# Moving the splits of w_out and the z weights to another stage, halving the z product, and laying out attention's buffers anew

## The chip, the core and the metric

The kernel runs on one core of a Trainium2 chip, as one launch. The metric is the device time in microseconds. A core has a matrix engine (TensorE, in the profile PE for its products and PEld for its weight loads), a vector engine (VectorE, DVE), a scalar engine (ScalarE, ACT), a general engine (GpSimd, POOL) and a fifth engine, SyncE (SP), whose queue in this kernel does little but issue DMA transfers. Each engine executes its own queue of instructions in the order written there, and waits at an instruction until what it needs is there. SBUF is the on-chip memory, in 128 partitions; PSUM is the small memory that takes the products of TensorE, in 8 banks of 128 x 512 fp32.

## What is computed

One hybrid decoder layer on x, 1024 rows of 1024 values in fp32, with a hidden width of 2816 in its two feed-forward networks:

```python
x = layer_norm(DN_ALPHA * x + 0.5 * swiglu(x, ffn1_wg, ffn1_wu, ffn1_wd), ln1_g, ln1_b)
proj = x @ w_in                                    # 3360 columns
(g_q, g_k, g_v, g_z, ..., n_q, n_kc, ..., n_gate) = jnp.split(proj, offsets, axis=-1)
o_gdn = gdn_mixer(g_q, g_k, g_v, g_z, ...)         # 4 heads of 128: ends in ... * silu(g_z)
o_nsa = nsa_mixer(n_q, n_kc, ...)                  # 8 query heads of 64, 2 key/value heads
mix = jnp.concatenate([o_gdn, o_nsa], axis=-1) @ w_out
x = layer_norm(DN_ALPHA * x + mix, ln2_g, ln2_b)
x = layer_norm(DN_ALPHA * x + 0.5 * swiglu(x, ffn2_wg, ffn2_wu, ffn2_wd), ln3_g, ln3_b)
```

swiglu(x) is (silu(x @ wg) * (x @ wu)) @ wd. The first mixer is a gated DeltaNet in chunks of 64 rows; g_z, 512 columns of the projection, only gates its output. The second is sparse attention with compressed, selected and windowed keys.

## The kernel before

**Products.** An fp32 operand is split into two parts, hi (a cast to the rounded type fp32r on ScalarE) and lo (the difference, on VectorE), and a product of two operands is three matmuls: hi x hi, hi x lo, lo x hi. `split` (line 100 the cast, 103 the difference) does this for the down products and the way out, `prep` (lines 290 and 291) for the weights of the gate and up products. A matmul here is 128 x 128 by 128 x 512.

**First feed-forward, gate and up** (`hidden`, 9 to 439 us in the profile). x @ wg and x @ wu are computed in pairs of 256 hidden columns, p from 0 to 10, with a scheme that needs seven half-size products instead of eight. A pair has a unit for gate and a unit for up; a unit has seven products of twelve matmuls (`u.do(n)`, line 302), in the order 1, 6, 2, 7, 5, 4, 3. A weight block of 1 MB comes by DMA into one of three buffers (`wring`); sums of its quarters are made on POOL or VectorE into eight `st` buffers; `prep` splits quarter or sum into `wh` and `wl`, of which there are seven buffers. Intermediate results live in twelve `ev` tiles of 128 x 512, products in the 8 PSUM banks. The hidden values go out to DRAM as `h`.

**First feed-forward, down** (`ffn`, 439 to 694 us). Again seven products, here n = 1, 6, 5, 3, 2, 7, 4, each over eleven p. For each p, `operands` loads two blocks of 256 KB, h and wd, into a ring of twelve `raw` tiles, splits them (`ah`, `al`, `bh`, `bl`, eight sets of buffers) and `mul` runs twelve matmuls over four banks (line 629). In the products 5, 3, 2 and 7, after every p with p % 4 == 1, one **job** is put in (line 664): twelve in all. A job loads a piece of the z columns of w_in (four jobs) or of w_out (eight), 128 x 1024, over POOL's DMA queue into `jr`, splits it into `jh` and `jl` (lines 100 and 103, line 139 for the scaled z weights), and sends the parts out to two DRAM scratches, `zw` and `wo`. All jobs share one set of buffers. The second feed-forward runs the same code without jobs (1951 to 2164 us).

**Projection, DeltaNet, keys** (694 to 1109 us) are not touched.

**Attention and way out** (`attend`, 1109 to 1506 us). Here TensorE's order is written by hand: units of attention, and between them steps of a **filler** at a given rate, `(24, 14, 13, 13)` steps for the first groups of rows. The first filler is `z_blocks`: g_z in four blocks of 128 columns, with both halves of the 1024 rows together, 64 steps of three matmuls (line 1036). Each block's weights are two tiles `zw` of 512 KB, reloaded when the step that used them last is written (line 1025); the results go to DRAM as `zT` (line 1049). After the last block `alloc_xT` takes the tiles that held x and 16 loads bring all of w_out's parts there, 8 MB. The further fillers are `tile_out(t)`, t from 7 down to 0: the way out for 128 rows, which loads the DeltaNet's part of `o`, `zT` and the residual (line 1063 for the first two), multiplies, splits into `oh` and `ol`, and runs 48 matmuls (line 1087) before the layer norm (line 756 is its last step, on POOL).

**Second feed-forward** (from 1516 us). It begins with transposes of the normalised rows (`acc`, line 230), 32 in the first group.

**What sets the order.** SP's queue issues nearly all transfers. Apart from TensorE in `attend` and some engines in the second feed-forward, a scheduler orders each engine's instructions from the program's text and its own costs. Buffers of a stage are laid out in SBUF in the order in which the pools are opened, and the next stage's pools take the same addresses; a tile of the new stage waits for whoever last used its place.

Of the kernel before, what the change touches and what calls it, by code (L numbers as in the profile page):

```python
# [36 lines left out]
class Ring:  # L37
# [5 lines left out]
    def tile(self, shape, dtype, name):  # L43
        pool, tag = next(self.rooms)
        return pool.tile(shape, dtype, name=name, tag=tag)


class Layer:
# [80 lines left out]
    def parts_of(self, src, hi, lo, scale=None):  # L129
        nc = self.nc  # L130

        def job(sb):
            raw = sb.tile([P, ND, P], F32, name="jr")
            nc.gpsimd.dma_start(raw, src)
            h, l = sb.tile([P, ND, P], F32R, name="jh"), sb.tile([P, ND, P], F32R, name="jl")
            if scale is None:
                self.split(h, l, raw)
            else:
                nc.scalar.mul(h, raw, scale)
                nc.vector.scalar_tensor_tensor(l, raw, scale, h.bitcast(F32), op0=ALU.mult, op1=ALU.subtract)  # L140
# [50 lines left out]
    def hidden(self, wg, wu, hd, cols, halves, rows, extra):  # L191
# [3 lines left out]
        with ExitStack() as st:  # L195
# [76 lines left out]
            class Unit:  # L272
# [15 lines left out]
                def prep(u, src, early=False):  # L288
                    h, l = [ev(0, [P, 4, P], F32R) if early else op.tile([P, 4, P], F32R, name=n) for n in ("wh", "wl")]
                    nc.scalar.copy(h, src)  # L290
                    nc.vector.tensor_tensor(l, src, h.bitcast(F32), op=ALU.subtract)  # L291
                    return h, l
# [239 lines left out]
            for p in range(1, NF // 2):  # L532
                g, v = nxt if p == 1 else (Gate(load(wg, p)), Up(load(wu, p)))
                v.gate, v.f = g, 2 * p
                finish = extra(ev()) if cols is None and p == 2 else None
                if p == 1:
                    g.adder = v.adder = nc.vector
                for u in (g, v):
                    for n in (1, 2, 6, 7, 5, 4, 3) if p == 1 else (1, 6, 2, 7, 5, 4, 3):
                        u.do(n)  # L540
                    if u is g and p == 1:
                        quarters()
                if finish is not None:
                    finish(bank())
                v.quarters()
# [7 lines left out]
    def ffn(self, wg, wu, wd, cols, halves, rows, extra, resid, name, tail=None, jobs=()):  # L553
# [3 lines left out]
        self.hidden(wg, wu, hd, cols, halves, rows, extra)  # L557
        with ExitStack() as st:
# [13 lines left out]
            jp, jobs = pool("dj", bufs=1) if jobs else None, list(jobs)  # L572
# [83 lines left out]
            def product(n, between=None):  # L656
                ps = banks()
                for p in range(NQ):
# [5 lines left out]
                    if jobs and n in (5, 3, 2, 7) and p % 4 == 1:  # L664
                        jobs.pop(0)(jp)
# [338 lines left out]
    def attend(self):  # L1004
# [4 lines left out]
        with ExitStack() as st:  # L1009
# [7 lines left out]
            self.zps, self.npo = pool("zps", bufs=2, space=PSUM), pool("npo", bufs=1, space=PSUM)  # L1017
            self.npt, self.nps = pool("npt", bufs=2, space=PSUM), pool("nps", bufs=3, space=PSUM)
            oT, fin = {}, {}

            def z_blocks():

                def load(b, k):
                    w = op.tile([P, 2, 4, P], F32R, name="zw", tag=("oh", "ol")[k], bufs=1)
                    nc.sync.dma_start(w.bitcast(F32), self.zw[b][:, k].bitcast(F32).rearrange("p i (k f) -> p i k f", f=P))
                    return w

                w = [load(0, k) for k in range(2)]
                for b in range(4):
                    pp = [self.zps.tile([P, 512], F32, name="pr") for _ in range(2)]  # L1030
                    for kc in range(ND):
                        h, l = [w[kc // 4][:, i, kc % 4] for i in range(2)]
                        for u in range(2):
                            xh, xl = self.xh[u][:, kc, :], self.xl[u][:, kc, :]
                            for i, (a, x) in enumerate(((h, xh), (h, xl), (l, xh))):
                                nc.tensor.matmul(pp[u], a, x, start=(kc == 0 and i == 0), stop=(kc == ND - 1 and i == 2))  # L1036
                            if u == 1 and kc % 4 == 3 and b < 3:
                                w[kc // 4] = load(b + 1, kc // 4)
                            yield
                        if b == 0 and kc in (1, 2):  # L1040
                            for br in range(2):
                                self.nsa_keys(1, br, kc - 1, nk.tile([P, 2, 512], F32R, name=f"ks{br}{kc - 1}"))
                    z = zp.tile([P, T], F32, name="z")
                    for u in range(2):
                        y = z[:, u * 512:u * 512 + 512]
                        nc.scalar.activation(y, pp[u], AF.Tanh)
                        nc.vector.scalar_tensor_tensor(y, y, 1.0, pp[u], op0=ALU.add, op1=ALU.mult)
                        nc.scalar.mul(y, y, self.nw)
                    nc.sync.dma_start(self.zT[b], z)

                self.alloc_xT()
                for k in range(0, ND, 2):
                    for u in range(2):
                        for i, x in enumerate((self.xh, self.xl)):
                            nc.sync.dma_start(x[u][:, k:k + 2, :].bitcast(F32), self.wo[i, u, k:k + 2].bitcast(F32).rearrange("k p c -> p k c"))
                yield

            def tile_out(t):
# [14 lines left out]
                else:  # L1073

                    oh = op.tile([P, ND, P], F32R, name="oh", tag="o", bufs=3)
                    ol = self.npp.tile([P, ND, P], F32R, name="ol", tag="pr", padded_shape=[P, 16, P], bufs=4)
# [4 lines left out]
                for u in range(2):  # L1081
                    cs = slice(u * 512, u * 512 + 512)
                    pp = self.zps.tile([P, 512], F32, name="pr")
                    ks = list(range(GH, ND)) + list(range(GH))
# [19 lines left out]
            def fill():  # L1104
                while filler:
# [68 lines left out]
            with tc.manual_schedule(engines={eng.PE}):  # L1174
# [10 lines left out]
                for t in reversed(range(NT)):  # L1185
                    if t + 2 < NT:
                        filler.append(tile_out(t + 2))
                    for kv in range(2):
# [4 lines left out]
                        run(us, (24, 14, 13, 13)[g - 1] / len(us) if g < 5 else 10 / len(us))  # L1193
# [24 lines left out]
    def first(self, x, wg, wu, wd, vecs, w_in, w_out):  # L1218
        nc = self.nc

        self.zw = self.scratch("zw", [4, P, 2, 2, 4 * P], F32R)
        self.wo = self.scratch("wo", [2, 2, ND, P, 512], F32R)
        jobs = [self.parts_of(w_in[:, C_Z + b * P:C_Z + (b + 1) * P].rearrange("(k p) f -> p k f", p=P),
                              self.zw[b][:, :, 0, :], self.zw[b][:, :, 1, :], 0.5) for b in range(4)]
        jobs += [self.parts_of(w_out[k * P:(k + 1) * P, :].rearrange("p (k f) -> p k f", f=P),
                               *[self.wo[i, :, k].rearrange("u p c -> p u c") for i in range(2)]) for k in range(ND)]
# [375 lines left out]
    def nsa_tile(self, i, kv, o):  # L1602
# [72 lines left out]
        def keyed(br, k0, masks, last):  # L1675
# [6 lines left out]
            def unit(k):  # L1682
# [6 lines left out]
                if h == 0:  # L1689
                    self.live += 1  # L1690
                    prs[j] = pp.tile([P, G, w], F32, name="pr", padded_shape=[P, G, 512], bufs=4)
# [119 lines left out]
```

## Time and profile before

| | before |
|---|---|
| median of 3 runs | 2174.02 us (2170.4 to 2177.31) |
| the profiled execution | 2175.48 us, its span 2173.8 us |
| mean granted TensorE clock | 0.987 |
| PE busy | 2081.2 us, 96% |
| PEld / DVE / ACT / POOL busy | 79% / 69% / 42% / 28% |

The profile is one execution. Times within it are microseconds from the start of the span. Busy shares are of the whole span, which has several stages with different limits, so a stage is read by itself. An arrow names whose work ended the wait: "ACT jh <- DMA jr" is ScalarE, about to write jh, waiting for the transfer into jr. The granted clock is that of TensorE, 1.00 being full speed.

### The profile page before, as it was taken

The numbers are of one execution on the slowest core, as the hardware profiler recorded it, in microseconds if no ns is written. First come the engines' busy times: TensorE is split into PE (matmuls) and PEld (weight loads), VectorE is DVE, ScalarE is ACT, GpSimd is POOL, SyncE is SP. The second block draws the span as 40 slices with busy tenths as digits, with TensorE's granted clock in tenths as the row PEclk, the third lists the DMA queues.
The fourth block names the chain that finished last, engine by engine and source line by source line (L and its number), as shares of the span: only waits on it lengthen the run. The fifth ranks groups of instructions, "written<-read, shape, count | busy, mean of one in ns | idle before, by whom it ended". The sixth has DMA issues, their size and how long they took to land.

```text
span 2173.8 us, 29550 instructions
## 1 busy us (share of the span) xinstructions
PE 2081.2 (96%) x10247; PEld 1714.3 (79%) x10247; DVE 1501.3 (69%) x2632; ACT 920.2 (42%) x1944; POOL 615.2 (28%) x644
## 2 busy tenths in 40 slices
PE   9999999998888998999999989998999999999998
PEld 7788888876667897888877767776778888887886
DVE  7966556577679747645457777774985656568998
ACT  5333323334343425335547756653633333334441
POOL 2545444111132103100013444442154444310011
PEclk9999999999999999999999999999999999999999
DMA  4333323298863544467451531222232323249761
GB/s 163 129 102 113 105 83 117 97 366 300 274 213 100 169 125 141 139 192 213 115 165 53 186 110 44 71 76 85 68 132 86 117 97 122 73 168 342 234 208 56
DMA packets 244472, 312.26 MB, mean 144 GB/s; under 512 B 24625, under 2 KB 149666, under 8 KB 244322
## 3 DMA queue, kind: packets, MB, share of 16 engines
q1 hardware_dynamic: 231330, 274.97, 39.0%
q0 software_dynamic: 12992, 35.39, 4.6%
q8 instruction: 81, 1.33, 0.3%
q14 instruction: 69, 0.57, 0.1%
HBM read 214.89 MB, written 93.32 MB: 142 GB/s over the span
## 4 chain that ended last, share of the span: by engine, by line
PE 46%; DVE 6%; issue 4%; DMA 3%; POOL 1%; ACT 1%; SPq 0%; POOLq 0%; DVEq 0%; ACTq 0%
PE bk L302 15%; PE dn L629 7%; PE pr L180 5%; PE pr L1087 3%; PE po L1633 3%; PE pt L1620 2%; PE pr L1036 2%; PE sc L1697 1%; PE sc L1696 1%; PE ga L1474 1%; PE ga L1484 1%; DVE wl L291 1%; DVE tl L1627 0%; DMA xl<-wo 0%; DMA zT<-zT 0%
## 5 line engine op out<-in xcount | busy, mean ns | idle before, releaser
L302 PE MATMUL bk<-x,wh 128*128 128x512 f32 x1040 | 321.5, 390 | 6.0 <-ACT wh L290 3.5
L629 PE MATMUL dn<-bl,ah 128*128 128x512 f32 x616 | 245.0, 398 | 24.8 <-DVE bl L103 24.8
L629 PE MATMUL dn<-bh,ah 128*128 128x512 f32 x616 | 243.3, 395 | 1.7 <-ACT bh L100 1.2
L629 PE MATMUL dn<-bh,al 128*128 128x512 f32 x616 | 242.9, 394 | 0.0
L302 PEld LDWEIGHTS bk<-x,wh 128*128 128x128 f32 x1040 | 194.3, 188 | 48.1 <-ACT wh L290 4.5
L290 ACT CAST wh<-st 128x512 fp32r<-128x512 f32 x176 | 108.6, 623 | 261.7 <-PE bk L302 215.7
L302 PE MATMUL bk<-acc,wh 128*128 128x512 f32 x704 | 217.0, 389 | 0.4 <-ACT ev L240 0.2
L302 PE MATMUL bk<-t,wh 128*128 128x512 f32 x704 | 217.2, 389 | 0.1
L302 PE MATMUL bk<-x,wl 128*128 128x512 f32 x520 | 202.8, 390 | 2.5 <-DVE wl L291 2.5
L359 POOL TENSOR_TENSOR ev<-ev 128x512 f32<-128x512 f32 x80 | 131.6, 1647 | 150.8 <-ACT wh L290 65.3
L629 PEld LDWEIGHTS dn<-bl,ah 128*128 128x128 f32 x616 | 117.8, 191 | 54.1 <-DVE bl L103 29.8
L290 ACT CAST wh<-wraw 128x512 fp32r<-128x512 f32 x130 | 80.6, 624 | 184.2 <-PE bk L302 166.3
L1730 POOL TENSOR_SCALAR pr<-pr,f 128x512 f32<-128x512 f32 (+3 forms) x192 | 106.7, 574 | 178.8 <-DVE f L1727 70.0
L285 POOL TENSOR_TENSOR st<-wraw 128x512 f32<-128x512 f32 x76 | 101.0, 1329 | 189.6 <-DVE wl L291 159.3
L302 PEld LDWEIGHTS bk<-t,wh 128*128 128x128 f32 x704 | 132.1, 188 | 28.3 <-DVE t L247 0.7
L302 PEld LDWEIGHTS bk<-acc,wh 128*128 128x128 f32 x704 | 132.0, 188 | 28.3 <-ACT ev L240 0.4
L1701 DVE TENSOR_REDUCE nm<-sc 128x1 f32<-128x512 f32 (+3 forms) x192 | 99.3, 520 | 75.2 <-PE sc L1699 68.8
L100 ACT CAST ah<-raw 128x512 fp32r<-128x512 f32 x154 | 95.1, 622 | 117.7 <-PE dn L629 57.8
L291 DVE TENSOR_TENSOR wl<-wraw,wh 128x512 fp32r<-128x512 f32 x130 | 115.3, 891 | 36.1 <-ACT wh L290 36.1
L629 PEld LDWEIGHTS dn<-bh,ah 128*128 128x128 f32 x616 | 117.6, 191 | 27.6 <-ACT bh L100 2.1
L629 PEld LDWEIGHTS dn<-bh,al 128*128 128x128 f32 x616 | 117.9, 191 | 24.4
L302 PE MATMUL bk<-t,wl 128*128 128x512 f32 x352 | 137.0, 389 | 0.0
(396 smaller groups left out, 4825.2 us busy)
## 6 DMA issues: line engine op xcount, KB each, us to landing
raw<-h SPq DMA_DIRECT2D x154, 256.0 KB
raw<-in_ffn_wd_dram SPq DMA_DIRECT2D x154, 256.0 KB
h<-ev SPq DMA_DIRECT2D x140, 256.0 KB
wraw<-in_ffn_wg_dram SPq DMA_DIRECT2D x20, 1024.0 KB
wraw<-in_ffn_wu_dram SPq DMA_DIRECT2D x20, 1024.0 KB
wraw<-in_w_in_dram SPq DMA_DIRECT2D x20, 512.0 KB
acc<-in_x_dram SPq DMA_DIRECT2D x32, 256.0 KB
qkvT<-cv SPq DMA_DIRECT2D x12, 512.0 KB
```

The costliest lines, as they stand in the source:

```text
L100: nc.scalar.copy(hi, src)
L180: nc.tensor.matmul(ps[half], ws[:, kc, :], xs[half][:, kc, :], start=(kc == 0 and i == 0), stop=(kc == ND - 1 and i == 2))
L285: (e or u.adder).tensor_tensor(t, a, b, op=o)
L290: nc.scalar.copy(h, src)
L291: nc.vector.tensor_tensor(l, src, h.bitcast(F32), op=ALU.subtract)
L302: nc.tensor.matmul(ps, w[:, kc, :], v[kc], start=(kc == 0 and i == 0), stop=(kc == 3 and i == 2))
L359: (nc.vector if u.f + 2 == NF else nc.gpsimd).tensor_tensor(t, t, u.gate.g[i, j], op=ALU.mult)
L629: nc.tensor.matmul(ps, a[:, t * P:(t + 1) * P], w, start=start and i == 0, stop=stop and i == 2)
L1087: nc.tensor.matmul(pp, a[:, kc, :], w[u][:, kc, :], start=(kc == ks[0] and i == 0), stop=(kc == ks[-1] and i == 2))
L1633: nc.tensor.matmul(po[0], v, w[:keys], start=(first and w is th[0]), stop=(last and w is tl[0]))
L1701: nc.vector.tensor_reduce(nm[:, j, h:h + 1], ps[:, :w], axis=AX.X, op=ALU.max, negate=True)
L1730: nc.gpsimd.tensor_scalar(prs[j][:, h, :], prs[j][:, h, :], f[:, j, h:h + 1], 1.0, op0=ALU.mult, op1=ALU.mult)
```

## The change

- **Jobs.** The twelve jobs become 24 of half the size (128 x 512): eight for the z weights, sixteen for w_out. They leave the down product and go into the gate and up products of the first feed-forward: from p = 3 on, after the products 6 and 5 of each unit, until none is left. They use SP's queue instead of POOL's, and their raw, hi and lo tiles are `ev` tiles, made by `prep`.
- **z.** g_z is computed in eight turns instead of four: the four column blocks for the first half of the rows, then again for the second half. Each turn reloads its two weight tiles, so there are 16 loads of 512 KB, not 8. The loads that the first attention groups need are placed after other steps, and the rates of the first groups become `(20, 15, 15, 14)`.
- **w_out.** When the turns of one half of the rows are done, x's tiles of that half are free, and eight loads for one column half of w_out are put on a list; one is issued with each filler step, and the rest before the first way-out matmuls.
- **Layout.** In `attend` the pools open in another order. The buffers of probabilities (`pr`, four) become four pools of their own, and `op` and `zp`, the way out's operands, come last in SBUF; in PSUM `zps` comes last and the three score banks are split into two pools.

The core of the diff:

```diff
     def parts_of(self, src, hi, lo, scale=None):
-        def job(sb):
-            raw = sb.tile([P, ND, P], F32, name="jr")
-            nc.gpsimd.dma_start(raw, src)
-            h, l = sb.tile([P, ND, P], F32R, name="jh"), sb.tile([P, ND, P], F32R, name="jl")
...
-            for d, t in ((hi, h), (lo, l)):
-                nc.gpsimd.dma_start(d, t.rearrange("p (u k) f -> p u (k f)", u=2))
+        def job(raw, prep):
+            nc.sync.dma_start(raw, src)
+            for d, t in zip((hi, lo), prep(raw, scale)):
+                nc.sync.dma_start(d, t.rearrange("p k f -> p (k f)").bitcast(F32))
...
                         u.do(n)
+                        if jobs and p > 2 and n in (6, 5):
+                            jobs.pop(0)(ev(None, [P, 4, P]), lambda raw, scale: u.prep(raw, True, scale))
...
-                    if jobs and n in (5, 3, 2, 7) and p % 4 == 1:
-                        jobs.pop(0)(jp)
...
-            op, zp = pool("op", bufs=2), pool("zp", bufs=2)
-            self.nsb, nk, self.nc1 = pool("nsb", bufs=2), pool("nk", bufs=1), pool("nc", bufs=1)
-            self.nqs, self.npp = pool("nqs", bufs=2), pool("np", bufs=1)
...
+            self.nsb, nk, self.nc1 = pool("nsb", bufs=2), pool("nk", bufs=1), pool("nc", bufs=1)
+            prs = [pool(f"pr{i}", bufs=1) for i in range(4)]
+            self.nqs, self.npp = pool("nqs", bufs=2), pool("np", bufs=2)
+            op, zp = pool("op", bufs=2), pool("zp", bufs=2)
...
+            def load_w(u):
...
+                for k in (4, 6, 0, 2):
+                    for i, x in enumerate((self.xh, self.xl)):
+                        loads.append(lambda i=i, x=x[u], k=k: nc.sync.dma_start(
+                            x[:, k:k + 2, :].bitcast(F32), self.wo[i, u, k:k + 2].rearrange("k p c -> p k c")))
...
-                for b in range(4):
-                    pp = [self.zps.tile([P, 512], F32, name="pr") for _ in range(2)]
+                for n in range(8):
+                    u, b = divmod(n, 4)
+                    pp = self.zps.tile([P, 512], F32, name="pr")
                     for kc in range(ND):
                         h, l = [w[kc // 4][:, i, kc % 4] for i in range(2)]
...
+                        if kc % 4 == 3 and n < 7:
+                            w[kc // 4] = load(n + 1, kc // 4)
+                        yield
...
+                    if b == 3:
+                        load_w(u)
...
             def fill():
+                if loads:
+                    loads.pop(0)()
...
-                        run(us, (24, 14, 13, 13)[g - 1] / len(us) if g < 5 else 10 / len(us))
+                        run(us, (20, 15, 15, 14)[g - 1] / len(us) if g < 5 else 10 / len(us))
```

**ScalarE, first down product, before** (`bh` and `ah` are the products' operands, `jh` a job's):

```order
L100 CAST bh<-raw 128x512
L100 CAST ah<-raw 128x512
L100 CAST bh<-raw 128x512
L100 CAST jh<-jr 128x1024
L100 CAST ah<-raw 128x512
L100 CAST bh<-raw 128x512
```

**ScalarE, first gate and up products, after** (`wh` are weights; an `ev<-ev` CAST is a job's split, COPY and ACTIVATE are the units' own):

```order
L284 CAST wh<-st 128x512
L284 CAST wh<-wraw 128x512
L310 COPY ev<-bk 128x512
L284 CAST wh<-st 128x512
L284 CAST wh<-wraw 128x512
L350 ACTIVATE ev<-ev 128x512
L284 CAST ev<-ev 128x512
L284 CAST wh<-st 128x512 x2
L350 ACTIVATE ev<-ev 128x512
L284 CAST wh<-wraw 128x512
L284 CAST ev<-ev 128x512
L350 ACTIVATE ev<-ev 128x512
```

A job's cast stood between the operands of the down product; a smaller one now stands between the weight casts of the gate and up products.

**SP's queue at the start of attention, before** (`qd` are queries that the stage before sends out, `zw` z's weights, `ks` and `qs` keys and queries):

```order
L845 DMA qd<-kl 64x1024
L1025 DMA zw<-zw 128x1024
L1063 DMA o<-od 128x4x128
L1610 DMA qs<-qd 128x4x128
L1599 DMA ks_9932<-kd 64x2x512 x2
L1599 DMA ks_9935<-kd 64x2x512 x2
L1599 DMA ks_9949<-kd 64x2x512 x2
L1599 DMA ks_9952<-kd 64x2x512 x2
L1025 DMA zw<-zw 128x1024 x2
L1049 DMA zT<-z 128x1024
```

**and after:**

```order
L1618 DMA qs<-qd 128x4x128
L1607 DMA ks_10045<-kd 64x2x512 x2
L1607 DMA ks_10048<-kd 64x2x512
L1036 DMA zw<-zw 128x1024
L1607 DMA ks_10048<-kd 64x2x512
L1607 DMA ks_10064<-kd 64x2x512 x2
L1607 DMA ks_10067<-kd 64x2x512 x2
L1036 DMA zw<-zw 128x1024
L1058 DMA zT<-z 128x512
L1036 DMA zw<-zw 128x1024 x2
L1058 DMA zT<-z 128x512
```

The first reload of z's weights stood behind all eight key loads; it now stands behind three.

**PE at the end of the way out, before** (`pr<-xh,oh` are way-out matmuls, `bk<-ident,acc` transposes for the second feed-forward, `bk<-x,ev` its first products):

```order
L1087 MATMUL pr<-xh,oh 128x512
L1087 MATMUL pr<-xl,oh 128x512
L1087 MATMUL pr<-xh,ol 128x512
L230 MATMUL bk<-ident,acc 128x128 x32
L302 MATMUL bk<-x_14578,ev 128x512
L302 MATMUL bk<-x_14579,ev 128x512
L302 MATMUL bk<-x_14578,ev 128x512 x3
```

**and after:**

```order
L1093 MATMUL pr<-xh,oh 128x512
L1093 MATMUL pr<-xl,oh 128x512
L1093 MATMUL pr<-xh,ol 128x512
L1093 MATMUL pr<-xh,oh 128x512
L223 MATMUL bk<-ident,acc 128x128 x28
L1093 MATMUL pr<-xl,oh 128x512
L1093 MATMUL pr<-xh,ol 128x512
L1093 MATMUL pr<-xh,oh 128x512
L1093 MATMUL pr<-xl,oh 128x512
L223 MATMUL bk<-ident,acc 128x128 x4
L1093 MATMUL pr<-xh,ol 128x512 x2
```

The transposes stood behind the last way-out matmul; 28 of them now stand 74 way-out matmuls ahead of the end, and the other four a little later.

More of the change, by code (lines that the diff above doesn't have):

```diff
@@ L182, in product, with hidden @@
         return ps
-    def hidden(self, wg, wu, hd, cols, halves, rows, extra):
+    def hidden(self, wg, wu, hd, cols, halves, rows, extra, jobs):
         nc, tc = self.nc, self.tc
@@ L556, in ffn @@
         hd = self.scratch(name, [NQ, 7, P, 512])
-        self.hidden(wg, wu, hd, cols, halves, rows, extra)
+        self.hidden(wg, wu, hd, cols, halves, rows, extra, list(jobs))
         with ExitStack() as st:
@@ new lines, in attend @@
+            self.zps = pool("zps", bufs=2, space=PSUM)
+            oT, fin = {}, {}
+            loads = []
+            def load_w(u):
+                for i, x in enumerate((self.xh, self.xl)):
+                    x[u] = self.xp[2 * i + u].tile([P, ND, 512], F32R, name=("xh", "xl")[i])
+                for k in (4, 6, 0, 2):
+                    for i, x in enumerate((self.xh, self.xl)):
+                        loads.append(lambda i=i, x=x[u], k=k: nc.sync.dma_start(
+                            x[:, k:k + 2, :].bitcast(F32), self.wo[i, u, k:k + 2].rearrange("k p c -> p k c")))
@@ L1031, in z_blocks @@
                     for kc in range(ND):
                         h, l = [w[kc // 4][:, i, kc % 4] for i in range(2)]
[L1033 to L1039, printed above, removed]
@@ L1049, in z_blocks @@
[L1049 to L1056, printed above, removed]
+                        xh, xl = self.xh[u][:, kc, :], self.xl[u][:, kc, :]
+                        for i, (a, x) in enumerate(((h, xh), (h, xl), (l, xh))):
+                            nc.tensor.matmul(pp, a, x, start=(kc == 0 and i == 0), stop=(kc == ND - 1 and i == 2))
@@ L1083, in tile_out @@
                     pp = self.zps.tile([P, 512], F32, name="pr")
+                    while loads:
+                        loads.pop(0)()
                     ks = list(range(GH, ND)) + list(range(GH))
@@ L1104, in fill @@
             def fill():
+                if loads:
+                    loads.pop(0)()
                 while filler:
@@ L1219, in first @@
         nc = self.nc
[L1221 to L1226, printed above, removed]
+        self.zw = self.scratch("zw", [4, P, 2, 2, 4 * P])
+        self.wo = self.scratch("wo", [2, 2, ND, P, 512])
+        jobs = [self.parts_of(w_in[k * 512:(k + 1) * 512, C_Z + b * P:C_Z + (b + 1) * P].rearrange("(k p) f -> p k f", p=P),
+                              self.zw[b][:, k, 0, :], self.zw[b][:, k, 1, :], 0.5) for b in range(4) for k in range(2)]
+        jobs += [self.parts_of(w_out[k * P:(k + 1) * P, u * 512:u * 512 + 512].rearrange("p (k f) -> p k f", f=P),
+                               self.wo[0, u, k], self.wo[1, u, k]) for u in range(2) for k in range(ND)]
         self.slot = {t: t for t in range(NT)}
```

49 lines of the change are left out of this document (24 added, 25 removed).

## The prediction

> **What bounds the kernel now.** I read the page's first part, then busy time by stretch, then the waits of the engine that is full, then who holds it up.
>
> ```profile
> span 2173.8 us, 29550 instructions
> PE 2081.2 (96%) x10247; PEld 1714.3 (79%) x10247; DVE 1501.3 (69%) x2632; ACT 920.2 (42%) x1944; POOL 615.2 (28%) x644
> ```
>
> TensorE (PE) is busy for 96% of the span, so time can come only from its idle 92.6 us and from stretches at a lower clock. Next, by stretch; the columns are start:end and length, busy us (and count) of PE, PEld, DVE, ACT and POOL, the granted clock, the DMA share, GB/s. In order: the first feed-forward's down product, the second's, attention with z, attention just after z, the start of the second gate and up products, the first gate and up products.
>
> ```profile
> 439.00:645.00 206.00, 180.80 (x752) 145.82 (x751) 146.70 (x236) 84.25 (x146) 33.25 (x47) 0.94 0.86 291
> 1951.00:2157.00 206.00, 204.67 (x898) 167.85 (x897) 190.30 (x319) 85.92 (x148) 13.38 (x14) 1.00 0.66 223
> 1109.00:1225.00 116.00, 114.57 (x639) 91.09 (x639) 77.28 (x183) 75.37 (x191) 34.74 (x58) 1.00 0.32 89
> 1225.00:1375.00 150.00, 137.96 (x786) 108.21 (x785) 111.77 (x271) 94.54 (x252) 66.35 (x106) 0.95 0.37 126
> 1506.00:1600.00 94.00, 81.48 (x382) 65.68 (x382) 80.89 (x120) 56.10 (x92) 20.94 (x15) 0.96 0.27 87
> 75.00:439.00 364.00, 364.00 (x1608) 301.46 (x1607) 230.07 (x327) 121.21 (x200) 150.26 (x106) 1.00 0.32 109
> ```
>
> The two down products are the same code on the same sizes, except that the first carries the jobs which split w_out and the z weights. For line 629's matmuls alone (PE, PEld, clock, DMA share, GB/s):
>
> ```profile
> 439.00:645.00 206.00, 180.49 (x749) 145.77 (x750) 0.94 0.86 291
> 1951.00:2157.00 206.00, 204.49 (x896) 167.85 (x897) 1.00 0.66 223
> ```
>
> In equal time the first does 749 matmuls, the second 896. At the second's pace, 206/896 = 0.230 us each, the missing 147 are worth 33.8 us. The waits of these stretches (total us, times, longest; the last line is the second product's) say who is late:
>
> ```profile
> PE dn L629 <- DVE bl L103: 23.5, 7, 7.3
> ACT jh L100 <- DMA jr<-in_w_out_dram: 69.0, 8, 12.2
> ACT jh L139 <- DMA jr<-in_w_in_dram: 22.5, 4, 9.0
> ...
> PE dn L629 <- DVE bl L103: 1.3, 3, 0.6
> ```
>
> ScalarE (ACT) stands 91.5 us in twelve waits, one per job, for the job's own load, while the operands that PE needs stand behind it. One of them, in order of time:
>
> ```profile
> 513.60 0.62 ACT L100 CAST bh<-raw 128x512 fp32r<-128x512 f32 x1
> 520.30 1.05 ACT L100 CAST jh<-jr 128x1024 fp32r<-128x1024 f32 x1 [6.08 <-DMA jr<-in_w_out_dram]
> 521.26 0.61 ACT L100 CAST ah<-raw 128x512 fp32r<-128x512 f32 x1
> ...
> 526.83 0.80 PE L629 MATMUL dn<-bl,ah 128*128 128x512 f32 x1 [7.26 <-DVE bl L103]
> 527.42 0.63 PE L629 MATMUL dn<-bh,al 128*128 128x512 f32 x1
> ...
> 530.37 0.39 PE L629 MATMUL dn<-bh,ah 128*128 128x512 f32 x1
> ```
>
> ACT stops, DVE follows, PE stops for 7.26 us, and the next eight matmuls take 3.54 us (526.83 to 530.37) where eight at 0.230 take 1.84: a long stop costs 1.7 us more at the lower clock.
>
> **The change, part by part.** *Jobs out of the down product.* Twelve loads, ACT splits of 1.05 us, DVE splits and 24 stores leave the stretch; PE's order there stays. The second product shows what remains: it has more DVE work (190.3 against 146.7 us) and no stall over 0.6. Bounds: nothing gained if the stalls come from the loads of h and wd alone, 33.8 + 2.5 (the second's own waits and slow starts) at most. I take **-33**, near the second product, because each long PE stop lies behind one of those ACT waits.
>
> *Jobs into the gate and up products.* 24 half-size jobs, each a load, an ACT split, a DVE split and two stores, four per pair of units. The rows that price them, and those that say how far ahead of PE the operands are (ACT's casts, what they waited for, PE's products, in 75 to 445 us):
>
> ```profile
> L290 ACT CAST wh<-wraw 128x512 fp32r<-128x512 f32 x55 | 34.3, 624 | 86.1 <-PE bk L302 81.9 <-DVE ev L349 2.1 <-DMA h<-ev 2.1
> L291 DVE TENSOR_TENSOR wl<-wraw,wh 128x512 fp32r<-128x512 f32 x57 | 50.3, 883 | 15.2 <-ACT wh L290 15.2
> L290 ACT CAST wh<-st x76: 610/624/629, 75.3 to 420.3; 128x512 fp32r<-128x512 f32 x76
>   PE bk L302: 189.6, 110
> L302 PE MATMUL bk<-x,wh x464: 389/389/477, 74.7 to 438.9; 128*128 128x512 f32 x155
> ```
>
> 24 x 0.624 = 15 us of ACT in 243 idle, 24 x 0.883 = 21 us of DVE in 134 idle. ACT's idle time is mostly waiting for PE to free a weight buffer (189.6 us): it is early, not late. Its last cast starts at 420.3; PE's last product, twelve matmuls, starts about 439.1 - 2.7 = 436.4, so the operands lead by some 15 us. A job stalls PE only when ACT or DVE is held that long. Behind a waiting job split stand the next casts and the copies that free PSUM banks; on SP's queue its stores stand ahead of the weight loads and the stores of h. Each weight tile has three buffers and a unit is 84 x 0.230 = 19 us, so a load late by a few us is not seen. DMA grows by 24 x 0.75 MB over six pairs of 39 us, 81 GB/s on 109. Cover: those 15 us. Without it each job would cost what one costs today, 33.8/12 = 2.8 us. Bounds 0 and 24 x 2.8 = 68; I take **+1**, as a 256 KB load is half of those that ACT waited 7.6 us on average for, and issued about 8 us ahead of its use.
>
> *z by halves.* The 192 z matmuls stay, but a 512 KB weight tile now serves four steps of three matmuls instead of eight, is loaded 16 times instead of 8, and has one buffer per half. The first reload is the tight one (a row of the chain of waits, then PE's and SP's timelines):
>
> ```profile
> 1090.88 3.89 DMA wraw<-in_w_in_dram
> ...
> 1109.29 0.48 PE L1036 MATMUL pr<-xh,zw 128*128 128x512 f32 x1
> 1115.34 0.37 SPq L1610 DMA_DIRECT2D qs<-qd  x1
> 1115.75 5.19 SPq L1599 DMA_DIRECT2D ks<-kd  x8
> 1121.07 6.35 SPq L1025 DMA_DIRECT2D zw<-zw  x2
> ...
> 1128.72 0.47 PE L1036 MATMUL pr<-xh,zw 128*128 128x512 f32 x1 [1.43 <-DMA zw<-zw]
> ```
>
> Today's reload is issued at 1121.07, behind eight ks loads, and used at 1128.72, 7.65 us later, 1.43 of it a stop. Now SP issues it after qs and three ks loads, 1115.75 + 3 x 0.65 = 1117.7. PE needs it after 38 wide matmuls, 1109.3 + 38 x 0.230 = 1118.0. Landing takes 3.9 (the 512 KB load of the first row) to 7.65 us, so PE stops for 3.6 to 7.4, plus 1.7 at the lower clock, less today's 1.43. With three ks loads ahead instead of eight I take a stop near the low end: +5. The next reloads have 16 wide matmuls and more, 4 to 6 us, on an emptier queue (share 0.32): +0.5 together. **+5.5**, bounds +1 and, if all 14 were short by 7.65 - 4.8 = 2.8 us, +39.
>
> By the Trainium skill ("DMA: Bandwidth & Descriptors", the section on the anatomy of one DMA) a transfer takes about 2.0 us plus its bytes at 436 GB/s, an estimate of 3.2 us for 512 KB, and the stop would be 2.9 us and this term about +1.5. Both rows above are longer, so the trace decides.
>
> *w_out in pieces.* A row of PE's waits in 1225 to 1375 us, and two rows of the chain:
>
> ```profile
> PE pr L1087 <- ACT oh L100: 3.1, 1, 3.1
> ...
> 1233.27 9.79 DMA xl<-wo
> 1243.08 9.64 DMA zT<-zT
> ```
>
> Today all 8 MB of w_out goes out when z ends, and the first way-out tile's z waits 9.64 us behind it; PE stops 3.1 us. Now half is loaded while z's second half runs and zT stands ahead of five of the other eight loads. -3.1 and -1.7 of lower clock: **-5**. What waits next are transposes for DVE's tl, unchanged. Bounds 0 and, were the stretch's whole loss gone, -12.
>
> *Way out's operands at the end of SBUF.* PE's timeline, with two rows of the chain for POOL and the DMA between:
>
> ```profile
> 1506.50 3.65 PE L230 MATMUL bk<-ident,acc 128*128 128x128 f32 x32
> 1509.50 2.12 POOL acc L756
> 1511.64 4.26 DMA wraw<-in_ffn_wg_dram
> 1516.59 7.42 PE L302 MATMUL bk<-x,ev 128*128 128x512 f32 x24 [6.44 <-ACT ev L290]
> ```
>
> The gate weights wait for the last row's normalisation, because their buffer lies where its tile was; PE stops 6.44 us and the next 24 matmuls take 7.3 instead of 24 x 0.230 = 5.5. Now the load stands before the last sw loads in SP's queue, the 32 transposes stand 74 way-out matmuls (17 us) before the end, and x11's and x21's splits run beside those. Late next: the transposes of the last tile, which need POOL's result 5.1 us after PE's end (1511.6 against 1506.5) and stand 14 matmuls, 3.2 us, after it: 1.9 us. -6.4 - 1.8 + 1.9 = **-6.3**; bounds -9 and 0.
>
> Sum: -33 + 1 + 5.5 - 5 - 6.3 = -37.8. The profiled execution took 2175.5 us (span 2173.8), 1.5 above the median of 2174.0; 2175.5 - 37.8 = 2137.7, against the median **2136**.
>
> **Rivals.** (1) *The down product keeps half its stalls*, because loads of h and wd at a DMA share of 0.86 are late too. For: DVE also waits for raw loads there. Against: the second product runs on the same loads. 2136 + 17 = 2153. (2) *Reloads of z starve PE* at most of 14 places, +39 - 5.5: 2136 + 33 = 2169, no change. For: 7.65 us against 4 to 6. Against: that row had 2 MB ahead of it. (3) *The jobs stall the gate and up products* as they stall the down product: a split waits for its load at the head of ACT's row until more than the 15 us lead is used up, again and again, at 2.8 us each: 2136 + 67 = 2203, slower. It decides from an average wait over about 5.6 us: per pair of 39 us ACT has some 25 idle, four jobs take 2.5, and (25 - 2.5)/4 = 5.6. For: the average today is 91.5/12 = 7.6 us. Against: that was at a share of 0.86, on twice the bytes; here it is 0.32.
>
> The Trainium skill's "TensorE: Matmul & The Clock Gate" (engine queue depths) calls ScalarE's and VectorE's queues strictly first in, first out, which is rival 3's rule; the cast at 521.26 right behind the job's agrees.
>
> **How the numbers follow.** Forecast 0.71 (own range 2122 to 2147), rival 1 0.12, rival 2 0.06, rival 3 0.06, something better than -52 us 0.05. The range 2122 to 2158 leaves out rivals 2 and 3, a little of rival 1 and the low end. A measurement here tells 0.3%, 6.5 us. Faster: 0.71 + 0.12 + 0.05 + 0.02 of rival 2 = 0.90; same 0.04; slower 0.06.
>
> **What would show it.** Right: line 629's matmuls in the first 206 us of the first down product near 896, no ACT wait for job loads there; the gate and up products still ending about 430 us after they began; one PE stop of 3 to 6 us at the first z reload; no stop at the first way-out tile; none of 6 us before the second gate product. Wrong: PE stops for ACT or DVE between 150 and 400 us, stops on zw at many places, or down-product stalls with no job in it.

## The result, and the profile after

| | before | after |
|---|---|---|
| median | 2172.82 us | 2137.58 us |
| range of 4 runs each | 2170.4 to 2177.31 | 2135.88 to 2138.58 |
| profiled execution (its span) | 2175.48 (2173.8) | 2137.25 (2135.3) |

The ratio of the times is 0.9835, 95% interval 0.9817 to 0.9853: the change saves about 35 us. Some executions of the kernels below took over 2200 us, a slow state, and are left out of all medians and ratios. The time is 1.6 us from the forecast of 2136, but the parts of the sum are not where it put them, as the stages show.

The first down product. One form of its matmuls in each kernel; the first and the last of the 308 are the two times near the end of the row, before:

```profile
L629 PE MATMUL dn<-bh,ah x308: 387/389/776, 439.3 to 692.9; 128*128 128x512 f32 x154
```

and after:

```profile
L627 PE MATMUL dn<-bh,ah x308: 389/389/478, 441.9 to 654.5; 128*128 128x512 f32 x154
```

Busy time by stretch of the first and the second down product:

```profile
442.00:648.00 206.00, 206.00 (x926) 170.67 (x925) 172.36 (x287) 93.61 (x161) 16.09 (x18) 1.00 0.64 217
1913.00:2119.00 206.00, 204.82 (x898) 168.02 (x898) 190.45 (x319) 85.81 (x148) 13.38 (x14) 1.00 0.65 223
```

ScalarE's longest waits in the first:

```profile
ACT ah L100 <- PE dn L627: 50.0, 31, 3.3
ACT ah L100 <- DMA raw<-h: 25.1, 13, 7.2
```

It takes 212.6 us instead of 253.6, 41.0 less. Line 627's matmuls alone are 893 in this stretch, against 749 before and 898 in the second product. PE is busy for all of the 206 us at full clock, and ScalarE now waits mostly for PE, so it is early again. The gate and up products, with the jobs in them (the last row is a job's cast):

```profile
L284 ACT CAST wh<-st 128x512 fp32r<-128x512 f32 x76 | 47.0, 622 | 98.3 <-PE bk L299 94.2 <-issue 3.2 <-DVE st L278 0.8
L284 ACT CAST ev<-ev 128x512 fp32r<-128x512 f32 x16 | 9.9, 617 | 5.4 <-DMA ev<-in_w_out_dram 5.4
```

The sixteen w_out jobs wait 5.4 us for their loads, all together. Set side by side, matmul by matmul and counted from the first one, the gate and up products lose 0.95 us against before, all of it within the first 120 of 1848 matmuls, before the first job, and the profile lists no stop of PE in 77 to 441 us. The jobs cost nothing there.

From the first z matmul to the end of the way out and on to the second down product, before:

```profile
L1036 PE MATMUL pr<-xh,zw x128: 387/393/500, 1109.3 to 1225.2; 128*128 128x512 f32 x128
L1087 PE MATMUL pr<-xh,oh x128: 389/397/792, 1243.1 to 1505.8; 128*128 128x512 f32 x128
L629 PE MATMUL dn<-bh,ah x308: 387/389/397, 1951.2 to 2162.8; 128*128 128x512 f32 x154
```

After, the same forms:

```profile
L1047 PE MATMUL pr<-xh,zw x128: 387/394/628, 1070.2 to 1191.3; 128*128 128x512 f32 x128
L1093 PE MATMUL pr<-xh,oh x128: 387/397/500, 1213.7 to 1472.0; 128*128 128x512 f32 x128
L627 PE MATMUL dn<-bh,ah x308: 387/389/398, 1912.6 to 2124.0; 128*128 128x512 f32 x154
```

Start of z to second down product: 841.9 us before, 842.4 after. Everything that the change does to attention came to nothing. It is not that nothing happened there; the stops moved. After, PE's timeline:

```profile
1075.91 0.47 PE L1704 MATMUL sc<-acc,qs 128*128 128x512 f32 x1 [2.51 <-DVE pc L1667]
1085.20 0.50 PE L1047 MATMUL pr<-xh,zw 128*128 128x512 f32 x1 [1.38 <-DMA zw<-zw]
1208.24 0.39 PE L1704 MATMUL sc<-acc,qs 128*128 128x256 f32 x1 [2.63 <-ACT pr L1710]
1477.37 0.73 PE L299 MATMUL bk<-x,ev 128*128 128x512 f32 x2 [1.82 <-ACT ev L284]
1494.74 0.74 PE L299 MATMUL bk<-x,wh 128*128 128x512 f32 x2 [3.05 <-ACT wh L284]
```

DVE's timeline:

```profile
1074.41 0.42 DVE L1665 TENSOR_REDUCE cnm<-sc 128x4 f32<-128x256 f32 x1 [4.48 <-issue]
```

ACT's timeline:

```profile
1206.89 0.62 ACT L100 CAST oh<-o 128x512 fp32r<-128x512 f32 x1 [2.97 <-POOL o L1071]
1476.70 0.62 ACT L284 CAST ev<-wraw 128x512 fp32r<-128x512 f32 x1 [16.02 <-DMA wraw<-in_ffn_wu_dram]
```

The stop of 3.13 us in the first way-out tile, 12 us behind that tile's first matmul, is gone. One of 2.63 stands 5 us ahead of the first way-out matmul, at a score that waits for ScalarE, which stands at the same `oh` split. The 6.44 before the second gate product is gone, and 1.82 and 3.05 stand behind a ScalarE that waited 16.02 us for wu. And there is a stop of 2.51 that nothing announced.

### The profile page after: what moved, and what is told of

Its sections match the earlier page's. It is cut to its first block, busy times and chain, and to the rows that moved or that the text cites. A ratio compares the mean times of both kernels' runs of the same rounds, so it can differ in the third digit from the quotient of the medians.

```text
span 2135.3 us, 29714 instructions
## 1 busy us (share of the span) xinstructions
PE 2074.9 (97%) x10247; PEld 1712.8 (80%) x10247; DVE 1514.9 (71%) x2644; ACT 923.0 (43%) x1956; POOL 586.4 (27%) x608
## 4 chain that ended last, share of the span: by engine, by line
PE 38%; DVE 5%; issue 3%; DMA 2%; POOL 1%; ACT 1%; POOLq 0%; SPq 0%; DVEq 0%; ACTq 0%
PE bk L299 16%; PE dn L627 8%; PE pr L1093 4%; PE po L1641 3%; PE pt L1628 3%; PE pr L1047 2%; PE sc L1705 1%; PE sc L1704 1%; DVE tl L1635 1%; POOL pr L1738 1%; DVE st L278 0%; DVE wl L285 0%; DMA ba<-in_ln_b_dram 0%; PE sc L1707 0%; DMA zw<-zw 0%
## 5 line engine op out<-in xcount | busy, mean ns | idle before, releaser
L627 PE MATMUL dn<-bl,ah 128*128 128x512 f32 x616 | 240.4, 390 | 1.2 <-DVE bl L103 1.2
L299 PE MATMUL bk<-acc,wl 128*128 128x512 f32 x352 | 136.9, 389 | 0.0
```

Of the source, the lines that this page charges most:

```text
L299: nc.tensor.matmul(ps, w[:, kc, :], v[kc], start=(kc == 0 and i == 0), stop=(kc == 3 and i == 2))
L627: nc.tensor.matmul(ps, a[:, t * P:(t + 1) * P], w, start=start and i == 0, stop=stop and i == 2)
```

## The experiments

### Which part of the change did it

**jobs_only** is the kernel before with the jobs moved and nothing else (the first of the four points under "The change").

> The kernel before with one part of the change alone: the 24 half-size jobs in the first gate and up products. Theory (the jobs cost the first down product what the curve of its matmuls shows, 254.4 us against 213.5 after the change, and cost nothing where they go): 2172.8 - 41 + 1 = 2133 us. Rival (the down product yields only the 33 us of the prediction's sum, the rest came from elsewhere): 2172.8 - 32 = 2141 us.

Ratio 0.9838 [0.9820, 0.9856], 35 us under before; the down product goes from 440.2 to 653.3, the same 213 us. **attend_only** is the other three points without the first.

> The kernel before with the rest of the change alone: z by halves, w_out in pieces, the new layout and rates; the twelve jobs stay in the down product. The prediction's three terms (+5.5, -5, -6.3) give 2172.8 - 5.8 = 2167 us. The two traces, from the first z matmul to the first matmul of the second down product, give 841.9 us before and 842.4 after: 2172.8 + 0.5 = 2173 us.

Ratio 1.0014 [1.0004, 1.0024]: slower by 3 us (0.9 to 5.2). So the moved jobs are the whole gain, and z by halves, w_out in pieces and the new layout together cost a little or nothing. About the attention part the two traces (+0.5) came nearer than the prediction's three terms (-5.8). The size of the jobs' term is less certain than the one pair of traces says: with the jobs in it, the down product took 253.6 us before and 249.2 in attend_only, and the median of jobs_only moved by 35, not 41.

### What in the jobs cost the down product its time

The prediction said: ScalarE stands in line for each job's own load. **load_ahead** issues that load one job earlier:

```diff
+                    if jobs and n == 6 and p == 8:
+                        ahead.append(jobs[0][0](jp))
                     if jobs and n in (5, 3, 2, 7) and p % 4 == 1:
-                        jobs.pop(0)(jp)
+                        jobs.pop(0)[1](jp, ahead.pop())
+                        if jobs:
+                            ahead.append(jobs[0][0](jp))
```

> The kernel before, jobs in the down product as before, but each job's load is issued when the job before it is split, one slot of about 11 us earlier; same work, same traffic, same buffers. Theory (the splits wait for their own loads at the head of ScalarE's and VectorE's queues, and the operands behind them are late): those waits go and most of the 41 us with them, 2135 to 2142 us. Rival (the jobs' traffic makes all loads of the down product late): no change, 2173 us.

Ratio 0.9994 [0.998, 1.0008], no change. But the waits had not gone either:

```profile
L633 PE MATMUL dn<-bh,ah x308: 387/389/775, 440.1 to 690.0; 128*128 128x512 f32 x154
```

ScalarE's waits:

```profile
ACT jh L100 <- DMA jr<-in_w_out_dram: 67.1, 8, 11.5
ACT jh L142 <- DMA jr<-in_w_in_dram: 16.9, 3, 8.7
```

84 us against 91.5. With one buffer a load waits for the split before it in any case, and in before it already left right behind that split; the edit moved next to nothing. The run tells nothing of the two theories. **no_split** leaves the splits out and keeps the bytes:

```diff
-            h, l = sb.tile([P, ND, P], F32R, name="jh"), sb.tile([P, ND, P], F32R, name="jl")
...
-            for d, t in ((hi, h), (lo, l)):
-                nc.gpsimd.dma_start(d, t.rearrange("p (u k) f -> p u (k f)", u=2))
+            for d, t in ((hi, raw), (lo, raw)):
+                nc.gpsimd.dma_start(d.bitcast(F32), t.rearrange("p (u k) f -> p u (k f)", u=2))
```

> The kernel before without the splits of the twelve jobs: each job loads its piece and sends it out twice unsplit, so the z weights and w_out are wrong in both parts, and the traffic is what it was. Theory (the loss is in the splits' waits on ScalarE and VectorE): about 41 us faster, 2132 us. Rival (the traffic): no change, 2173 us; in between if both share it.

2154.4 us in one execution, in between:

```profile
L623 PE MATMUL dn<-bh,ah x308: 387/389/628, 442.6 to 672.6; 128*128 128x512 f32 x154
```

ScalarE's longest wait:

```profile
ACT ah L100 <- DMA raw<-h: 46.3, 24, 7.9
```

230.0 us, 23.6 less than before, and 17.4 more than without jobs: ScalarE now waits for the product's own operand h. The bytes are the same, but the packets are not: the stores now write plain fp32, where they wrote the rounded type fp32r, and move in fewer packets. GpSimd's queue over the whole run (packets, MB, share of the DMA engines' time), before:

```profile
q0 software_dynamic: 12992, 35.39, 4.6%
```

and in no_split:

```profile
q0 software_dynamic: 9920, 35.39, 4.4%
```

That is 128 packets fewer for each of the 24 stores, so the traffic that is left is a little lighter than that of before. **split_on_pool** keeps loads, splits and stores, and gives the splits to GpSimd:

```diff
-                self.split(h, l, raw)
...
+            if scale is not None:
+                nc.gpsimd.tensor_scalar(raw, raw, scale, None, op0=ALU.mult)
+            nc.gpsimd.tensor_copy(h, raw)
+            nc.gpsimd.tensor_tensor(l, raw, h.bitcast(F32), op=ALU.subtract)
```

> The kernel before, jobs in the down product with the same loads, stores and buffers, but split by GpSimd, whose queue carries no operand of the down product. Theory now (of the 41 us, some 24 lie in the splits' waits on ScalarE and VectorE, the 230.8 us of the down product without splits against 254.4; the other 17 in the jobs' traffic, 230.8 against 213.5): down product about 231 us, 2172.6 - 23 = 2150 us. Rival one (all of it is traffic, and leaving out the splits changed something else): 2172 us. Rival two (all of it is the waits): 2133 us.

Ratio 1.002 [1.0004, 1.0036]: nothing gained, with no job on ScalarE or VectorE at all. The same form of matmuls first:

```profile
L628 PE MATMUL dn<-bh,ah x308: 387/389/632, 441.8 to 694.3; 128*128 128x512 f32 x154
```

ScalarE's longest wait:

```profile
ACT ah L100 <- DMA raw<-h: 74.9, 25, 9.1
```

POOL's timeline:

```profile
508.80 2.71 POOL L139 TENSOR_TENSOR jl<-jr,jh 128x1024 fp32r<-128x1024 f32 x1
575.66 8.87 POOL L138 CAST jh<-jr 128x1024 fp32r<-128x1024 f32 x1 [7.42 <-DMA jr<-in_w_out_dram]
```

DVE's timeline:

```profile
509.18 2.88 DVE L103 TENSOR_TENSOR bl<-raw,bh 128x512 fp32r<-128x512 f32 x1
```

The groups of DVE's instructions:

```profile
L103 DVE TENSOR_TENSOR al<-raw,ah 128x512 fp32r<-128x512 f32 x63 | 52.8, 839 | 3.9 <-ACT ah L100 3.9
```

ScalarE's waits for jr are gone and 74.9 us of waits for h stand in their place. But this isn't a clean answer either: VectorE, which makes the operands that PE waits for, is slower beside the busy GpSimd, its subtraction 839 ns on average where it took 702 before. **three_ahead** keeps the splits on ScalarE and VectorE, as 24 halves with the loads three jobs ahead:

```diff
+            raw = sb.tile([P, 4, P], F32, name="jr", bufs=4)
...
-                    if jobs and n in (5, 3, 2, 7) and p % 4 == 1:
-                        jobs.pop(0)(jp)
+                    if jobs and n in (5, 3, 2, 7) and p % 2 == 0:
+                        if jobs[3:]:
+                            ahead.append(jobs[3][0](jp))
+                        jobs.pop(0)[1](jp, ahead.pop(0))
```

> The kernel before with the jobs in the down product, but as 24 halves whose loads are issued three jobs (some 16 us) ahead into four buffers; same splits on ScalarE and VectorE, same bytes over GpSimd's queue. If the splits' waits for their loads cost some 24 of the 41 us and the jobs' traffic 17: ScalarE no longer waits for jr, the down product takes about 231 us and the kernel 2150 us. If all is traffic: 254 us and 2173 us, with waits for h in place of the waits for jr. If all is waits: 214 us and 2133 us.

Ratio 1.0026 [1.001, 1.0042], down product 252.0 us:

```profile
L633 PE MATMUL dn<-bh,ah x308: 387/389/676, 440.1 to 692.1; 128*128 128x512 f32 x154
```

Some of ScalarE's waits:

```profile
ACT jh L142 <- DMA zw<-jh: 19.4, 4, 7.1
ACT jh L100 <- DMA wo<-jh: 18.6, 6, 5.4
ACT jh L100 <- DVE bl L103: 14.8, 3, 6.5
ACT jh L100 <- DVE jl L103: 11.6, 4, 4.9
ACT jh L142 <- DMA jr<-in_w_in_dram: 3.3, 1, 3.3
```

Of the waits for jr one of 3.3 us is left. But ScalarE stands at the jobs' splits no less than before: 38 us for the stores of the job before, which must leave the one `jh` buffer, and most of the rest behind VectorE. All its waits there add up to 90.7 us, against 91.5. The run changed the reason and left the wait, so it doesn't tell what the wait is worth. Two more runs put the old jobs back beside the moved ones, half of each at a time: **add_loadsplit** loads and splits, **add_traffic** loads and stores. Of the edit, the first two lines are the one's, the next two the other's, the last two stand in both:

```diff
+            h, l = sb.tile([P, ND, P], F32R, name="jh"), sb.tile([P, ND, P], F32R, name="jl")
...
+                self.split(h, l, raw)
...
+            for d, t in ((hi, raw), (lo, raw)):
+                nc.gpsimd.dma_start(d, t.rearrange("p (u k) f -> p u (k f)", u=2))
...
+                    if more and n in (5, 3, 2, 7) and p % 4 == 1:
+                        more.pop(0)(jp)
```

> The changed kernel, with the twelve old jobs put back into the down product beside the moved ones, as loads and splits whose results go nowhere: all of the waits, a third of the jobs' traffic. Against the changed kernel's 2137.6 us: waits and traffic as 24 and 17: 2137.6 + 24 + 6 = 2167 us. All traffic: 2137.6 + 41/3 = 2151 us. All waits: 2137.6 + 41 = 2178 us.

> The changed kernel, with the twelve old jobs put back into the down product as loads and unsplit stores to a place that nobody reads: all of the jobs' traffic, none of the waits of ScalarE and VectorE. Waits and traffic as 24 and 17: 2137.6 + 17 = 2155 us. All traffic: 2178 us. All waits: 2137.6 us.

As in no_split, add_traffic's stores are plain fp32 (9920 packets on GpSimd's queue). The same two views of add_loadsplit:

```profile
L643 PE MATMUL dn<-bh,ah x308: 387/389/632, 439.6 to 666.3; 128*128 128x512 f32 x154
```

ScalarE's longest wait:

```profile
ACT jh L100 <- DMA jr<-in_w_out_dram: 40.3, 7, 9.1
```

and of add_traffic:

```profile
L639 PE MATMUL dn<-bh,ah x308: 387/389/628, 440.7 to 664.8; 128*128 128x512 f32 x154
```

ScalarE's longest wait:

```profile
ACT ah L100 <- DMA raw<-h: 46.9, 21, 8.0
```

add_loadsplit: 2152.5 us, ratio 0.9902 [0.9876, 0.9927]; add_traffic: 2149.0 us, 0.9883 [0.9865, 0.9902]; the changed kernel 0.9835. The down products together, with the time that ScalarE stood idle before the jobs' splits:

| what the down product carries beside its own work | first to last matmul, us | ScalarE's waits at the jobs' splits, us |
|---|---|---|
| nothing (after; jobs_only) | 212.6; 213.1 | none |
| loads and unsplit stores (add_traffic; no_split) | 224.1; 230.0 | none |
| loads and splits (add_loadsplit) | 226.7 | 64.6 |
| all three (before; attend_only; load_ahead) | 253.6; 249.2; 249.9 | 91.5; 89.5; 88.4 |
| all three, loads three jobs ahead | 252.0 | 90.7 |
| all three, splits on GpSimd | 252.5 | none, but VectorE slower |

Traffic alone costs 11.5 to 17 us, loads and splits 14, and all three 36 to 41, more than the 26 to 31 of both, although both counts hold the loads. So neither the waits of ScalarE nor the traffic is the cause by itself, as the 91.5 us in the profile of before seemed to say: take away what ScalarE waits for, and it waits for the next thing that is late.

One link between the two can be read. The last number of these rows is the median time from a load's issue to its landing, before:

```profile
jr<-in_w_out_dram POOLq DMA_DIRECT2D x8, 512.0 KB, 8.1
```

and in add_loadsplit, without the stores:

```profile
jr<-in_w_out_dram POOLq DMA_DIRECT2D x8, 512.0 KB, 4.8
```

Beside the stores a job's load lands later, and ScalarE stands longer at its split, 91.5 us instead of 64.6. Whether this, and the larger number of packets of the split stores, make up the whole excess is not shown. A version with all the bytes and all the splits, but no job's wait in ScalarE's queue and no slower VectorE, was not among the runs. Nor was one that sends the jobs of the down product over SP's queue: the change moved them to another stage and another queue at once, and no run separates the two.

### What the attention part lost

**ol_ring** moves one tile of the changed kernel, the lo operand of the last way-out tile:

```diff
-                    ol = prs[0].tile([P, ND, P], F32R, name="ol", tag="pr", padded_shape=[P, 16, P])
+                    ol = op.tile([P, ND, P], F32R, name="ol", tag="o", bufs=3)
```

> The changed kernel, with the lo operand of the last way-out tile in the third buffer of the o tiles instead of the first pr buffer, whose place the second weight buffer (wu) of the next stage takes. Theory (ScalarE's 16 us wait for wu holds back the copies behind it and makes the stops of 1.8 and 3.1 us after the way out): both stops and the low clock behind them go, 2137.6 - 4 = 2133.6 us. Rival (the transposes of the last normalised tiles are as late as wu, and the stops stay): 2137.6 us.

2131.7 us, ratio 0.9811 [0.9793, 0.9828]; its runs, 2128.4 to 2134.6 us, all lie below those of the changed kernel. wu's load leaves before the last way-out tile, and ScalarE's two casts run without a wait, ahead of the end of the way out at 1475:

```profile
1452.58 0.93 SPq L253 DMA_DIRECT2D wraw<-in_ffn_wu_dram  x2
```

ACT's timeline:

```profile
1463.54 1.14 ACT L284 CAST ev<-wraw 128x512 fp32r<-128x512 f32 x2
```

From the first gate matmul of the second feed-forward to its down product it takes 434.3 us instead of 439.9, as before the change (434.6). **ring_direct** adds the direct z:

```diff
+                    if u:
+                        nc.gpsimd.tensor_copy(last[0][:, b, :], z[:, 3 * P:])
...
-                zT = op.tile([P, GH, P], F32, name="zT", bufs=1)
+                zT = last[0] if t == NT - 1 else op.tile([P, GH, P], F32, name="zT", bufs=1)
```

> As the run before it, and for the first way-out tile z goes straight from the on-chip result to the tile's operand, with four copies on GpSimd, instead of out to DRAM and back. Theory (the 2.6 us stop of the scores before the first way-out tile comes from ScalarE standing at that tile's split, which waits for z): 2133.6 - 3 = 2130.6 us. Rival (w_out's loads take its place as what is late): 2133.6 us.

2127.5 us, ratio 0.9797 [0.9778, 0.9817], the fastest of all. The stop of 2.6 us is gone. Its runs, 2126.1 to 2132.1 us, overlap those of ol_ring, so what this second step adds is not clear of the noise. **cnm_moved** adds an exchange of two pools:

```diff
-            self.nsb, nk, self.nc1 = pool("nsb", bufs=2), pool("nk", bufs=1), pool("nc", bufs=1)
+            self.nsb, self.nc1, nk = pool("nsb", bufs=2), pool("nc", bufs=1), pool("nk", bufs=1)
```

> The kernel with the o-tile operand and the direct z, with one thing more: the softmax's small tiles (cnm and others) lie 16 KB lower, off the place of kh, which is still being stored to DRAM when attention begins. Theory (VectorE's first cnm waits 4.5 us for that store, and PE stops 2.5 us behind it and runs on at the lower clock): 2127.5 - 4 = 2123.5 us. Rival (PE then reaches the first reload of z's weights earlier and waits there instead): 2127.5 us.

2130.6 us, ratio 0.9794 [0.9777, 0.9811]: no change. PE's timeline in ring_direct:

```profile
1076.33 0.47 PE L1708 MATMUL sc<-acc,qs 128*128 128x512 f32 x1 [2.51 <-DVE pc L1671]
1085.66 0.79 PE L1047 MATMUL pr<-xh,zw 128*128 128x512 f32 x1 [2.41 <-DMA zw<-zw]
```

DVE's timeline in cnm_moved:

```profile
1073.95 0.43 DVE L1669 TENSOR_REDUCE cnm<-sc 128x4 f32<-128x256 f32 x1 [0.46 <-PE sc L1666]
```

and PE's:

```profile
1093.64 0.55 PE L1047 MATMUL pr<-xh,zw 128*128 128x512 f32 x1 [4.64 <-DMA zw<-zw]
```

The theory holds for the place, since VectorE's wait of 4.5 us and PE's of 2.5 are gone, and the rival for the time: PE gets to a reload of z's weights sooner and stops 4.64 us there, instead of 2.51 and 2.41. The reload is what bounds the start of attention. **whole_z** takes the halves and pieces out of the changed kernel (the z_blocks and the rates of before in it):

> The changed kernel with z computed over all rows at once, w_out loaded after z, and the rates of before; the new layout and the moved jobs stay. By the prediction's terms (halves +5.5, pieces -5): 2137.6 - 0.5 = 2137 us. By the stage times of the traces (from the first z matmul to the last of the way out, without the moved transposes: 392.5 to 397.9 us with z whole, 398.2 and 399.0 by halves): 2137.6 - 2.8 = 2135 us.

Ratio 0.9838 [0.9813, 0.9864], not to be told from the changed kernel. It has a stop of 2.53 in the first way-out tile, and its wait for wu is 15.7 us, so the layout brings that with either z. From the first z matmul to the last of the way out it takes 405.3 us (1069.7 to 1475.0) against 401.8 in the changed kernel.

## Why the prediction was right, and where it was wrong

The time, 2136 for 2137.6, is that near by luck: one term was too small, the other three promised 5.8 us together that did not come, and the two errors cancelled.

*Jobs out of the down product, -33.* The right direction, and the whole of the gain; measured 36 to 41 between traces, where 36.3 was the bound, and 35 in the medians. The working compared the first 206 of some 254 us and left out the rest, where another stop of 3.35 us stood (at 664). The step that falls short is "each long PE stop lies behind one of those ACT waits", taken as the cause. It is a part of it: without the splits the down product is 23.6 us shorter. But in the trace of before the three longest of these waits (10.5, 12.2 and 11.1 us, ending at 541, 592 and 619) have no PE stop of over 1 us in the 10 us behind them, so a wait of ScalarE is not yet a stop of PE, and in add_loadsplit 64.6 us of such waits go with a loss of only 14. three_ahead says nothing against the step, since ScalarE stood at the splits as long as before; split_on_pool, which frees ScalarE of them, gains nothing, but slows VectorE. The number came from comparing two executions of one code, with and without the jobs, and that comparison didn't depend on the story. Rival 1's reason, the traffic, is another part of the cause, 11.5 to 17 us by itself; its time did not come because the bytes left with the jobs.

*Jobs into the gate and up products, +1.* Right, at zero: the jobs there wait 5.4 and 2.7 us, and the operands led by some 15. Rival 3 is out.

*z by halves, +5.5.* From the first z matmul to the last of the way out, 396.5 us became 401.8, and 3.65 of the 5.3 are the transposes that moved there; halves and pieces together cost 1.6 by this pair, not 0.5 (whole_z points the other way, and neither is clear of the noise). The mechanism was right, but the stop at the first reload was 1.38 (2.41 in ring_direct), because PE had just stopped 2.51 for something else: the new layout puts the softmax's first small tile, `cnm`, on the place of `kh`, which is being stored to DRAM, and cnm_moved, which takes it off that place, doesn't have the stop. There a reload costs 4.64, the size that the term had. No term asked what the new layout puts under attention's first tiles. The +1.5 beside this term leaves out the 1.7 and the 0.5 that the term itself adds, and with them would be +3.7. The section of the Trainium skill's "DMA: Bandwidth & Descriptors" from which its 3.2 us come gives its fit for transfers that GpSimd issues. z's loads go over SP's queue, and the first reload was issued at 1078.04 and used, after the stop, at 1085.20, 7.2 us later.

*w_out in pieces, -5.* Wrong. The chain from z through DRAM to the `oh` split was shortened by too little; ScalarE stands 2.97 us at that split, and the scores behind it in its queue are late. "What waits next" was named as the transposes for DVE's tl; it was ScalarE at the same split.

*Operands at the end of SBUF, -6.3.* Wrong. From the last way-out matmul to the second down product 445.4 us became 440.6, and 3.65 of these 4.8 are the 32 transposes that now stand in the way out: 1.1 gained. The step priced wg's load alone, and the new layout exchanged the two loads. SP's queue, before (the last way-out matmuls start at 1506):

```profile
1491.40 1.13 SPq L260 DMA_DIRECT2D wraw<-in_ffn_wu_dram  x2
1511.64 0.92 SPq L260 DMA_DIRECT2D wraw<-in_ffn_wg_dram  x2
```

and after (they start at 1472):

```profile
1444.69 0.93 SPq L253 DMA_DIRECT2D wraw<-in_ffn_wg_dram  x2
1472.86 0.93 SPq L253 DMA_DIRECT2D wraw<-in_ffn_wu_dram  x2
```

Before, wu left ahead of the end and wg behind it; after, wg leaves early and wu, whose buffer now lies on the last way-out tile's `ol`, behind the end, and ScalarE waits 16 us for it. ol_ring shows it.

## What to carry to other kernels

A wait with a large total in an engine's row names what is late first, not what its removal is worth; compare the stage with the same code without the suspect, over the whole stage, remove the suspect in more than one way, and see in the trace that it is gone: three_ahead took away a row and not the wait. When buffers change place, list for each first tile of the new stage what lay there and when it is let go, for every tile and not only for the one that the change speaks of: moving one tile and keeping one result on the chip were worth 8 to 10 us together, the whole attention part of this change nothing.

## What the runs showed of the hardware

GpSimd and VectorE slowed each other in the down product of split_on_pool. With GpSimd splitting the jobs, VectorE's 128x512 subtraction took 839 ns on average instead of 702, and up to 2.88 us. They took turns: that subtraction of 2.88 us began at 509.18, 0.4 us into GpSimd's own subtraction of 2.71 us, and ended 0.55 us behind it. The other way round, GpSimd's cast of 128x1024, 1.04 to 1.5 us in nine places of twelve, took 8.87 and 9.07 us in two where VectorE ran its 128x512 operations with hardly a gap. The Trainium skill ("GPSIMD Engine Reference", section 1, Specifications) says that the two share SBUF interfaces and contend where a VectorE instruction has two SBUF inputs, as this subtraction has; the trace agrees, and gives the price.

Equal DMA shares also were not equal harm: in 439 to 645 us, the down product but for its end, add_traffic moved 303 GB/s at a share of 0.84 and PE did 874 instructions; before, with the splits and with more and smaller packets on GpSimd's queue, moved 291 GB/s at 0.86 and PE did 752. The stretch in add_traffic:

```profile
439.00:645.00 206.00, 198.00 (x874) 161.59 (x873) 164.03 (x271) 88.69 (x152) 39.58 (x54) 0.99 0.84 303
```
